# Softmax times values on one core: the values' spreads moved into the first two heads of a pass, and the last head's load cut into 2, 2, 2, 1, 1 rows

## The chip, the cores and the metric

One core of one Trainium2 chip (trn2). The metric is the device time of one execution in microseconds (us). It is somewhat longer than the span of the profile (first to last instruction): by 1.7 to 2.8 us in the runs of this study.

## The reference

```python
def setup_inputs():
    batch, n_heads, seq, head_dim = 8, 12, 1024, 64
    return {"scores": randn(batch, n_heads, seq, seq) float32,      # 403 MB
            "v": randn(batch, n_heads, seq, head_dim) float32}

def reference(scores, v):
    scores_max = np.max(scores, axis=-1, keepdims=True)
    attn = np.exp(scores - scores_max)
    attn = attn / (np.sum(attn, axis=-1, keepdims=True) + 1e-8)
    return np.matmul(attn, v).astype(np.float32)
```

96 heads, each a 1024 x 1024 block of scores and 1024 x 64 values.

## The kernel before

The program is a loop of 24 passes over four heads (numbered 0 to 3). A head has eight "rows" (`r`); a row is 128 queries by 1024 keys, and all eight lie in one buffer of 4 MB. For a row, ScalarE (ACT) takes the exponential (two rows in one instruction, one at a time for the last two rows of a pass), TensorE (PE) transposes eight 128 x 128 blocks into PSUM (the memory that it writes to), VectorE (DVE) copies them to SBUF (the core's working memory) (the "row copy", L273), and TensorE multiplies the eight blocks with the values and a column of ones (two rows later in the program). After four or eight rows DVE takes the reciprocals of the sums and multiplies. GpSimd (POOL) casts the values of four heads to 16 bits once per pass; DVE then *spreads* them, in four copies per head, into the layout that TensorE reads. The loop, abridged (`...` and the comments stand for what is left out):

```python
def heads(n0):
    for k in range(AHEAD):                     # four heads of a pass
        if k == 0:
            for s in range(S):                 # head 0's own four spreads
                spread_v(k, s)
        ...
        for r in range(R):                     # eight rows
            if r % EB == 0:
                ...                            # exp of two rows, ACT, L255
            psT = take(psT_bufs)               # four buffers
            for c in range(C):
                nc.tensor.transpose(...)       # PE, L267
            pt = take(pt_bufs)                 # four buffers
            copy = nc.vector.tensor_copy(out=pt[:], in_=psT[:])      # DVE, L273
            if k < AHEAD - 1 and r % (R // S) == 0:
                spread_v(k + 1, r // (R // S), copy)                 # DVE, L207
            if r == R - 1:
                load_next(k, n0)
            pending.append((n0, k, r, pt, st))
            if len(pending) > LAG:             # LAG = 2
                finish(pending.pop(0))         # PE, L145; DVE, L124 and L129
    while pending:
        finish(pending.pop(0))
    cast_v()                                   # POOL, L203
    last(n0)                                   # loads of heads 2, 3 and the values; store

# in last(), the last but one pass:
load(AHEAD - 2, BH - 2, (4, 4))
load(AHEAD - 1, BH - 1, (4,))
store(n0, AHEAD - T)
load(AHEAD - 1, BH - 1, (2, 1, 1), 4)
```

All transfers are issued by one queue (SP), in this order.

The softmax here doesn't subtract the row's maximum and nothing guards it: scores larger than these inputs give would overflow.

Of the kernel before, what the change touches and what calls it, by code (L numbers as in the profile page):

```python
# [14 lines left out]
def kernel(  # L15
# [12 lines left out]
    BH = B * H  # L28
    assert SQ % P == 0 and SK % P == 0
    R = SQ // P  # L30
# [5 lines left out]
    AHEAD = 4  # L36
    Q = P // AHEAD
    S = P // Q
# [54 lines left out]
    def take(bufs):  # L93
        k = turn.get(id(bufs), 0)
        turn[id(bufs)] = k + 1
        return bufs[k % len(bufs)]
# [4 lines left out]
    def after(a, b):  # L101

        tc.add_manual_dep(
            a.ins,
            b.ins.name,
            mybir.DependencyInfo(mybir.DependencyClass.NoSync, mybir.DependencyReason.DATA),
            reason="order",
        )

    def queue(dma):  # L110

        if queued:
            after(dma, queued[-1])
        queued.append(dma)

    def one(bh, n):
        return bh[bass.ds(n, 1)].rearrange("o p r d -> (o p) r d")

    def normalise(k, st, first, last):

        psO = psO_whole if k % 2 == 0 else psO_banks[first]
        psO = psO[:, :, 0 : G * M].rearrange("p b (g m) -> p b g m", m=M)
        recip = st["recip"][:, first:last]
        nc.vector.reciprocal(out=recip, in_=psO[:, :, :, D : D + 1])  # L124
        h = k % T
        for t in range(T):
            part = slice(t * W, (t + 1) * W)
            rows = st["out_sb"][h * W : (h + 1) * W, t, first * G : last * G, :]
            nc.vector.tensor_tensor(  # L129
                out=rows.rearrange("j (b g) d -> j b g d", g=G),  # L130
                in0=psO[part, :, :, 0:D],
                in1=recip[part].to_broadcast([W, last - first, G, D]),
                op=mybir.AluOpType.mult,
            )

    def finish(u):

        n0, k, r, pt, st = u
        b, g = r // G, r % G
        if r == 0:  # L140
            st["recip"] = take(rc_bufs)
            st["out_sb"] = out_bufs[k // T]
        bank = psO_whole[:, b] if k % 2 == 0 else psO_banks[b][:, 0]
        for c in range(C):
            nc.tensor.matmul(  # L145
                out=bank[:, g * M : (g + 1) * M],
                lhsT=pt[:, c * P : (c + 1) * P],
                rhs=st["vones"][:, c, 0:M],
                start=(c == 0),
                stop=(c == C - 1),  # L150
            )
        if k % 2 == 1:
            if g == G - 1:
                normalise(k, st, b, b + 1)
        elif r == R - 1:
            normalise(k, st, 0, R // G)
        if r == R - 1 and k == T - 1:
            store(n0, 0)

    def store(n0, k):  # L160

        rows = out_bh.rearrange("(m x) y -> m x y", x=P)
        dma = nc.sync.dma_start(
            out=rows[bass.ds((n0 + k) // T, 1)].rearrange("o x y -> (o x) y"),
            in_=out_bufs[k // T][:].rearrange("x t r d -> x (t r d)"),
        )
        for other in stores:
            apart(dma, other)
            apart(other, dma)
        apart(dma, dma)  # L170
        stores.append(dma)
        queue(dma)
# [8 lines left out]
    def load(k, n, parts=(R,), r=0, **cond):  # L181
        for rows in parts:
            queue(
                nc.sync.dma_start(  # L184
                    out=s_bufs[k][:, r : r + rows, :],
                    in_=one(sc_bh, n)[:, r : r + rows, :],
                    **cond,
                )
            )
            r += rows  # L190

    def load_v(n):

        rows = v_bh.rearrange("(m x) y -> m x y", x=P)
        queue(
            nc.sync.dma_start(  # L196
                out=v_sb[:].rearrange("x h s l d -> x (h s l d)"),
                in_=rows[bass.ds(n // AHEAD, 1)].rearrange("o x y -> (o x) y"),
            )
        )  # L200

    def cast_v():
        nc.gpsimd.tensor_copy(out=v_half[:], in_=v_sb[:])  # L203

    def spread_v(k, s, behind=None):

        copy = nc.vector.tensor_copy(  # L207
            out=vones_bufs[k][s * Q : (s + 1) * Q, :, 0:D].rearrange(
                "i (h l) d -> i h l d", l=L
            ),  # L210
            in_=v_half[k * Q : (k + 1) * Q, :, s],
        )
        if behind is not None:
            after(copy, behind)

    def load_next(k, n0):

        if k < AHEAD - 2:
            load(k, (n0 + (AHEAD + k)) % BH, cond=n0 < BH - AHEAD)

    def last(n0):


        before = queued[-1:]

        with tc.If(n0 < BH - 2 * AHEAD) as cmp:  # L226
            queued[:] = before
            load(AHEAD - 2, (n0 + (2 * AHEAD - 2)) % BH)
            load_v((n0 + 2 * AHEAD) % BH)
            load(AHEAD - 1, (n0 + (2 * AHEAD - 1)) % BH)  # L230
            store(n0, AHEAD - T)
        with cmp.Else():
            with tc.If(n0 < BH - AHEAD) as cmp2:
                queued[:] = before
                load(AHEAD - 2, BH - 2, (4, 4))
                load(AHEAD - 1, BH - 1, (4,))
                store(n0, AHEAD - T)
                load(AHEAD - 1, BH - 1, (2, 1, 1), 4)
            with cmp2.Else():
                queued[:] = before  # L240
                store(n0, AHEAD - T)

    def heads(n0):

        for k in range(AHEAD):
            if k == 0:
                for s in range(S):
                    spread_v(k, s)
            st = dict(vones=vones_bufs[k])
            for r in range(R):  # L250
                if r % EB == 0:
                    p_nat = take(p_bufs)
                    rows = 1 if k == AHEAD - 1 and r == R - EB else EB
                    for g in range(0, EB, rows):
                        nc.scalar.activation(  # L255
                            out=p_nat[:, g : g + rows, :].rearrange(
                                "p r (x v) -> p x r v", v=Q * L
                            ),
                            in_=s_bufs[k][:, r + g : r + g + rows, :].rearrange(
                                "p r (i x l) -> p x (r i) l", i=Q, l=L  # L260
                            ),
                            func=EXP,
                        )
                p_row = p_nat[:, r % EB, :].rearrange("p (h q l) -> p h l q", q=P, l=L)
                psT = take(psT_bufs)
                for c in range(C):
                    nc.tensor.transpose(  # L267
                        out=psT[:, c * P : (c + 1) * P],
                        in_=p_row[:, c // L, c % L, :],
                        identity=order16[:],  # L270
                    )
                pt = take(pt_bufs)
                copy = nc.vector.tensor_copy(out=pt[:], in_=psT[:])  # L273
                if k < AHEAD - 1 and r % (R // S) == 0:
                    spread_v(k + 1, r // (R // S), copy)
                if r == R - 1:
                    load_next(k, n0)
                pending.append((n0, k, r, pt, st))
                if len(pending) > LAG:
# [3 lines that stand above are left out]
        cast_v()  # L283
        last(n0)

    assert BH % AHEAD == 0 and BH >= 2 * AHEAD and SK == Q * S * C
# [5 lines left out]
    with tc.For_i(0, BH, AHEAD, iteration_sync="reg_based") as n0:  # L292
        queued.clear()
        heads(n0)
# [30 lines left out]
```

## Time and profile before

| | before |
|---|---|
| time, median of the first 3 runs | 1065.58 us (1065.39 to 1066.23) |
| span of the profiled run | 1064.0 us |
| bytes moved | 453 MB, 99.2% of 16 DMA engines' span |
| start of ACT on head 1 of the last pass | 1030.12 us |
| end of the last multiply | 1059.19 us |

I call the 29.06 us (of the unrounded times) between the last two rows the *tail*. It starts with the landing of head 1's scores (ACT waits for it). The prediction shows the page and the main views and how they are read. One more view is needed later, DVE's waits in the tail (columns: who waits, for whom, us in total, times, the longest):

```profile
DVE recip L124 <- PE psO L145: 0.7, 1, 0.7
DVE pt L273 <- PE L145: 0.2, 1, 0.2
DVE pt L273 <- PE psO L145: 0.2, 1, 0.2
```

### The profile page before, as it was taken

What the parts mean: (1) busy time and instruction counts of PE and PEld (TensorE: products, weight loads), DVE (VectorE), ACT (ScalarE), POOL (GpSimd) and SP (SyncE); (2) the same over time, 40 slices, a digit from 0 to 9 for tenths busy, and PEclk for the clock granted to TensorE, in tenths of its full rate; (3) what the DMA queues carried; (4) which work ended last, traced back from release to release, by engine and by line L of the source; (5) the groups of instructions that cost most, each with busy time, mean ns of one, the idle gap of its engine ahead of it and who ended that gap; (6) DMA issues with size and microseconds to landing.
All of it is one profiled execution on the core that took longest, in us unless ns stands there. A gap on an engine that the chain in (4) does not pass through costs nothing.

```text
span 1064.0 us, 32161 instructions
## 1 busy us (share of the span) xinstructions
PE 731.4 (69%) x12288; PEld 678.4 (64%) x12288; DVE 786.6 (74%) x1589; ACT 735.6 (69%) x432; POOL 48.1 (5%) x31
## 2 busy tenths in 40 slices
PE   2766766767766677677686776867666777666676
PEld 2665756667666667666575665767565666666675
DVE  3776876868768777677786776868768687687777
ACT  3766776666767668586676866667766668676685
POOL 0000000000000000000000000000000000000000
PEclk9888888878889888888988888888889788898989
DMA  9999999999999999999999999999999999999995
GB/s 397 431 418 434 426 433 434 433 434 432 432 434 432 425 443 430 429 431 428 433 431 436 432 434 434 431 434 424 441 427 434 432 426 435 432 432 428 440 425 236
DMA packets 24772, 453.06 MB, mean 426 GB/s; under 512 B 2752, under 2 KB 2752, under 8 KB 9152
## 3 DMA queue, kind: packets, MB, share of 16 engines
q1 hardware_dynamic: 24768, 453.00, 99.2%
q8 instruction: 4, 0.07, 0.0%
HBM read 436.21 MB, written 25.17 MB: 434 GB/s over the span
## 4 chain that ended last, share of the span: by engine, by line
DMA 81%; ACT 12%; issue 3%; ACTq 1%; PE 1%; DVE 0%; SPq 0%; PEld 0%; DVEq 0%
DMA s_nat<-in_scores_dram 81%; ACT p_nat L255 12%; PE psT L267 1%; ACTq L255 1%; ACTq L226 0%; ACTq L292 0%; PE psO L145 0%; DVE pt L273 0%; PE psO_whole L145 0%; SPq L184 0%; PEld L267 0%; ACTq L320 0%; DVE out_sb L129 0%; SPq L196 0%; PEld L145 0%
## 5 line engine op out<-in xcount | busy, mean ns | idle before, releaser
L255 ACT ACTIVATE p_nat<-s_nat 128x2048 f16<-128x2048 f32 (+1 forms) x408 | 704.8, 1799 | 228.1 <-DMA s_nat<-in_scores_dram 202.2
L267 PE MATMUL psT<-order,p_nat 128*128 128x128 f16 x6144 | 574.9, 246 | 269.9 <-ACT p_nat L255 263.9
L273 DVE COPY pt<-psT 128x1024 f16<-128x1024 f16 x768 | 515.8, 687 | 200.6 <-PE L267 109.4
L267 PEld LDWEIGHTS <-p_nat 128*128 128x128 f16 x6144 | 446.5, 123 | 298.3 <-ACT p_nat L255 295.7
L145 PEld LDWEIGHTS <-pt 128*128 128x128 f16 x6144 | 302.9, 107 | 81.0 <-DVE pt L273 77.7
L145 PE MATMUL psO<-vones,pt 128*128 128x65 f16 x3072 | 177.4, 201 | 53.9 <-DVE pt L273 50.2
L145 PE MATMUL psO_whole<-vones,pt 128*128 128x65 f16 x3072 | 189.9, 211 | 2.7 <-DVE pt L273 2.4
L207 DVE COPY vones<-v_half 32x512 f16<-32x512 f16 x384 | 109.4, 285 | 22.8 <-POOL v_half L203 6.0
L255 ACT ACT_TABLE_LOAD x24 | 30.8, 1283 | 89.8 <-DMA s_nat<-in_scores_dram 81.7
L203 POOL CAST v_half<-v_sb 128x2048 f16<-128x2048 f32 x25 | 47.4, 1896 | 1002.3 <-DVE vones L207 957.1
L129 DVE TENSOR_TENSOR out_sb<-psO,recip 64x256 f32<-64x256 f32 x192 | 81.1, 423 | 6.1
L129 DVE TENSOR_TENSOR out_sb<-psO_whole,recip 64x512 f32<-64x512 f32 x96 | 66.1, 688 | 3.0
L124 DVE RECIPROCAL recip<-psO 128x4 f32<-128x4 f32 x96 | 17.1, 178 | 34.4 <-PE psO L145 17.6
L124 DVE RECIPROCAL recip<-psO_whole 128x8 f32<-128x8 f32 x48 | 9.7, 203 | 4.5 <-PE psT L267 3.9
L71 DVE MEMSET vones<- 128x16 f16 x4 | 0.2, 72 | 0.8 <-PEq L309 0.8
L62 DVE CAST order<-ident 128x128 f16<-128x128 f32 x1 | 0.2, 227 | 0.4 <-POOL ident masks.py:199 0.4
masks.py:199 POOL TENSOR_SCALAR_AFFINE_SELECT ident<-ident 128x128 f32<-128x128 f32 x1 | 0.3, 295 | 0.1
masks.py:197 POOL MEMSET ident<- 128x128 f32 x1 | 0.2, 205 | 0.3 <-POOLq L309 0.3
L309 POOL MEMSET const-float32-0.0<- 128x1 f32 x1 | 0.1, 100 | 0.2 <-issue 0.2
L309 POOL MEMSET const-bfloat16-1.0<- 128x1 bf16 x1 | 0.1, 103 | 0.0
L309 POOL MEMSET const-uint8-127<- 128x1 uint8 x1 | 0.1, 103 | 0.0
L309 POOL MEMSET const-float32-1.0<- 128x1 f32 x1 | 0.1, 100 | 0.0
## 6 DMA issues: line engine op xcount, KB each, us to landing
s_nat<-in_scores_dram SPq DMA_DIRECT2D x96, 4096.0 KB, 35.8
v_sb<-in_v_dram SPq DMA_DIRECT2D x24, 1024.0 KB, 33.1
out_dram<-out_sb SPq DMA_DIRECT2D x48, 512.0 KB, 26.9
s_nat<-in_scores_dram SPq DMA_DIRECT2D x3, 2048.0 KB, 32.4
s_nat<-in_scores_dram SPq DMA_DIRECT2D x1, 1024.0 KB, 25.4
s_nat<-in_scores_dram SPq DMA_DIRECT2D x2, 512.0 KB
```

The lines of the kernel that those rows point to most:

```text
L62: nc.vector.tensor_copy(out=order16[:].rearrange("p (t j) -> p t j", t=T), in_=ident32[:].rearrange("p (j t) -> p t j", t=T),)
L71: nc.vector.memset(vo[:, :, D : D + 2], 1.0)
L124: nc.vector.reciprocal(out=recip, in_=psO[:, :, :, D : D + 1])
L129: nc.vector.tensor_tensor(out=rows.rearrange("j (b g) d -> j b g d", g=G), in0=psO[part, :, :, 0:D], in1=recip[part].to_broadcast([W, last ...
L145: nc.tensor.matmul(out=bank[:, g * M : (g + 1) * M], lhsT=pt[:, c * P : (c + 1) * P], rhs=st["vones"][:, c, 0:M], start=(c == 0), stop=(c ...
L203: nc.gpsimd.tensor_copy(out=v_half[:], in_=v_sb[:])
L207: copy = nc.vector.tensor_copy(out=vones_bufs[k][s * Q : (s + 1) * Q, :, 0:D].rearrange("i (h l) d -> i h l d", l=L), in_=v_half[k * Q : ( ...
L255: nc.scalar.activation(out=p_nat[:, g : g + rows, :].rearrange("p r (x v) -> p x r v", v=Q * L), in_=s_bufs[k][:, r + g : r + g + rows, :] ...
L267: nc.tensor.transpose(out=psT[:, c * P : (c + 1) * P], in_=p_row[:, c // L, c % L, :], identity=order16[:],)
L273: copy = nc.vector.tensor_copy(out=pt[:], in_=psT[:])
L309: nc = _bacc.Bacc("TRN2", target_bir_lowering=False, num_devices=1)
```

## The change

It wants to finish with the cast values earlier (so that the next cast and the next load of the values aren't held), to unload DVE in the last heads of a pass, and to let ACT start earlier on the very last head.

```diff
-                load(AHEAD - 1, BH - 1, (4,))
+                load(AHEAD - 1, BH - 1, (2,))
                 store(n0, AHEAD - T)
-                load(AHEAD - 1, BH - 1, (2, 1, 1), 4)
+                load(AHEAD - 1, BH - 1, (2, 2, 1, 1), 2)
...
-                if k < AHEAD - 1 and r % (R // S) == 0:
-                    spread_v(k + 1, r // (R // S), copy)
+                if k < 2 and r < 6:
+                    spread_v(1 + (k * 6 + r) // S, (k * 6 + r) % S, copy)
```

## The prediction

> **What bounds the kernel now.** I read the page first: the DMA row and the queue table, because 81% of the chain of work that ended last is one transfer, the load of the scores.
>
> ```profile
> DMA  9999999999999999999999999999999999999995
> GB/s 397 431 418 434 426 433 434 433 434 432 432 434 432 425 443 430 429 431 428 433 431 436 432 434 434 431 434 424 441 427 434 432 426 435 432 432 428 440 425 236
> q1 hardware_dynamic: 24768, 453.00, 99.2%
> DMA s_nat<-in_scores_dram 81%; ACT p_nat L255 12%; PE psT L267 1%; ACTq L255 1%; ACTq L226 0%; ACTq L292 0%; PE psO L145 0%; DVE pt L273 0%; PE psO_whole L145 0%; SPq L184 0%; PEld L267 0%; ACTq L320 0%; DVE out_sb L129 0%; SPq L196 0%; PEld L145 0%
> ```
>
> The reader is to see that 39 of 40 slices of the DMA row are full, at some 432 GB/s, and that only the last slice (26.6 us) is not. A pass over four heads moves 16.78 MB of scores, 1.05 MB of values and 1.05 MB of results, 18.87 MB; at 432 GB/s that is 43.7 us. The chain repeats at that distance (its long DMA pieces start at 405.63, 449.34 and 493.02 us). So 23 of the 24 passes are as long as their bytes.
>
> Second, busy time by stretch: one steady stretch, the end of the loads, and the tail.
>
> ```profile
> 500.00:544.00 44.00, 31.06 (x522) 28.84 (x520) 32.82 (x67) 30.91 (x19) 1.90 (x1) 0.85 1.00 430
> 1020.00:1046.00 26.00, 19.65 (x354) 17.69 (x352) 22.93 (x50) 23.28 (x14) 0.00 (x0) 0.93 0.99 425
> 1046.00:1064.00 18.00, 8.80 (x176) 7.69 (x176) 12.03 (x24) 7.50 (x5) 1.90 (x1) 0.87 0.35 145
> ```
>
> After the window come PE, PEld, DVE, ACT and POOL busy us, the clock, the DMA share and GB/s. In the steady stretch DVE is busy 32.8 of 44 us, so it has 11 us to spare per pass while DMA has none. In the last 18 us DMA is 35% busy: only here can compute set the end.
>
> Third, who waits on the issuing queue, to see what an earlier release could buy.
>
> ```profile
> SPq L184 <- ACT p_nat L255: 273.4, 47, 13.1
> SPq L163 <- DVE vones L207: 238.4, 23, 10.6
> SPq L196 <- POOL v_half L203: 97.3, 23, 5.6
> v_sb<-in_v_dram SPq DMA_DIRECT2D x24, 1024.0 KB, 33.1
> ```
>
> The load of the values waits for the cast, 4.2 us per pass (97.3/23). But that load lands 33.1 us after its issue (last row, from the table of DMA issues), while its own 1.05 MB is 2.4 us of transfer: it stands behind about 30 us of queued work. Issuing it 4 us earlier doesn't move its place in the queue.
>
> Fourth, the timeline of the end, of DVE, of ACT and of the queue.
>
> ```profile
> 1045.96 7.59 ACT L255 ACTIVATE p_nat<-s_nat 128x2048 f16<-128x2048 f32 x5 [1.14 <-DMA s_nat<-in_scores_dram]
> ...
> 1046.91 0.29 DVE L207 COPY vones<-v_half 32x512 f16<-32x512 f16 x1
> 1047.23 1.29 DVE L273 COPY pt<-psT 128x1024 f16<-128x1024 f16 x2
> 1048.55 0.29 DVE L207 COPY vones<-v_half 32x512 f16<-32x512 f16 x1
> 1048.87 1.90 DVE L273 COPY pt<-psT 128x1024 f16<-128x1024 f16 x3
> 1050.80 0.21 DVE L124 RECIPROCAL recip<-psO_whole 128x8 f32<-128x8 f32 x1
> ...
> 1056.69 0.69 DVE L273 COPY pt<-psT 128x1024 f16<-128x1024 f16 x1
> 1058.10 0.18 DVE L124 RECIPROCAL recip<-psO 128x4 f32<-128x4 f32 x1 [0.72 <-PE psO L145]
> 1058.31 0.88 DVE L129 TENSOR_TENSOR out_sb<-psO,recip 64x256 f32<-64x256 f32 x2
> ```
>
> ACT starts on the last head at 1045.96, 1.14 us after it was free, when the first four rows have landed, and then runs without a gap to 1053.55. DVE is behind it: from 1034.73 to 1057.38 it runs instruction after instruction with about 30 ns between them at most. The waits of DVE from 1032.8 on sum to 1.1 us, of which 0.7 us is the wait for the very last matmuls. So in the tail the end is set by DVE's backlog and not by ACT.
>
> **What the Trainium skill says.** "DMA: Bandwidth & Descriptors", Where 436 GB/s comes from, puts the ceiling of the 16 SBUF ports at 435.2 GB/s. The slices here read 424 to 443 with a mode of 432 to 434: the trace agrees, and there is nothing left to win in the steady loop. The same page, Queues, rings and completion order, says each DMA engine consumes descriptors in ring order; the 33.1 us of a 1 MB load agree. "Perfetto Trace Analysis", DMA Optimizations, says that splitting a transfer may let work start sooner if the DMA engines are generally idle. Here they are full, so a split can only reorder landings. "VectorE: DVE Perf Modes", The DRAIN you can't avoid, has the next operation wait until the pipe is empty unless it isn't held. Both are seen: back-to-back copies of the transposed rows start 0.61 us apart though one lasts 0.69, and a spread that stands between two of them stretches the distance to 1.03 us (1046.20 to 1047.23), so it costs 0.42 us there, and 0.32 us behind a multiply.
>
> **The change part by part.** *Spreads.* Nothing is removed: 12 copies of 32x512 at 0.285 us (109.4 us/384) remain per pass. Four each behind rows 0, 2, 4, 6 of heads 0, 1 and 2 become six each behind rows 0 to 5 of heads 0 and 1. In the steady loop this takes no time off the bound. The cast can run some 8 us earlier, until it meets the landing of its input (issued 966.59, landed 999.73; the cast ran at 1008.19). Gain: 0.
>
> In the last pass it counts. DVE has short waits in head 0 (0.25, 0.19 and 0.19 us before three row copies, 0.63 in all); the two extra spreads there cost 2 x 0.42 = 0.84 us, so about 0.2 us is carried into head 1. From head 1's first row copy (1032.82) to the end, eight spreads become six. Before, by their places: head 1 0.35 + 0.32 + 0.42 + 0.32, head 2 0.32 + 0.32 + 0.42 + 0.42, together 2.89 us. After: 0.35, about 0.25 (a wait of 0.16 us absorbs part), 0.32, and three at 0.42, 2.18 us. Saved 0.71 us, less the 0.2 carried in: 0.5 us at the end.
>
> *Parts of the last head.* In the last but one pass the load goes from 4, store, 2, 1, 1 rows to 2, store, 2, 2, 1, 1: same bytes, same last part. The first two rows land one 1 MB transfer (2.4 us) earlier, at about 1043.4 in place of 1045.86; ACT is busy with head 2 until 1044.82, so it starts 1.1 us earlier. Rows 2 and 3 land behind the store, where the store landed before (1047.19): ACT starts on them at 1047.2, against 1047.78. Rows 4 and 5 land as before (1049.63), where ACT started on them at 1049.74. So ACT meets the same landings from there and ends within 0.1 us of 1053.55. What this part buys is that DVE is not held at the head's first rows: before, row 0's transposes ended 0.65 us ahead of its copy (1048.83 against 1049.48), about the shift the spreads bring. It makes that shift safe and adds at most 0.1 us. One more transfer costs one issue of 0.33 us, 20 us ahead of the landing.
>
> Sum: 0.5 to 0.6 us off 1065.58, that is 1065.0.
>
> **The rivals.** (1) No effect at all: PE paces the tail, not DVE. With no spreads in head 2, DVE would copy seven rows in a row at 0.61 us, while PE needs about 0.70 us for a row's transposes and matmuls (1029.02, 1029.72, 1030.43 in head 0). For it: PE's lead in head 2 is only 0.3 to 1.6 us. Against: every copy there started within 30 ns of DVE becoming free. It would give 1065.3 to 1065.6.
> (2) The steady loop gets shorter, because the values' load no longer waits 4.2 us on the cast: 23 passes at even 1 us would be 1042. Against: the queue never runs dry, at 99.2%.
> (3) Six spreads in heads 0 and 1 make DVE late, so ACT frees the scores' buffers later and the loads are issued later. For it: head 0 also has its own four spreads. Against: DVE's 11 us spare per pass, and 25 us of queued transfers that hide a late issue. It would show as slices under 9 in the DMA row and a few us; I give it one chance in a hundred.
> (4) The store behind two rows in place of four makes a dry queue in the last but one pass. Against: the store was issued at 1023.68 while head 1 landed only at 1030.02 and two halves of head 2 still stood before it.
>
> **Range and chances.** The mechanism is worth 0 to 1 us; the three runs of before spread over 0.84 us (1065.39 to 1066.23), and the median of another kernel's runs moves by about as much. Predicted 1065.0, 8 in 10 between 1064.2 and 1065.9. Two per cent is 21 us, more than the whole tail: faster 0.005, same 0.99, slower 0.005.
>
> **What would show it right or wrong.** Right: DMA share about 99% and 43.7 us between passes as before; the queue's wait on the cast gone or far below 97 us; ACT starting on the last head near 1044.9 but ending near 1053.5; DVE's last row copy near 1056.1 in place of 1056.69. Wrong: that copy at its old place with DVE idle in the last two heads (PE paces, rival 1); ACT ending much earlier (the last rows land earlier than I hold); passes of another length (rivals 2 and 3).

## The result

| | before | changed |
|---|---|---|
| time, median of 6 runs | 1065.68 us (1065.39 to 1066.23) | 1066.65 us (1065.74 to 1067.01) |
| span of the profiled run | 1064.0 us | 1064.4 us |
| ACT starts on head 1 / head 3 of the last pass | 1030.12 / 1045.96 | 1030.52 / 1045.10 |
| ACT's end | 1053.55 | 1053.90 |
| last row copy / last multiply's end | 1056.69 / 1059.19 | 1057.38 / 1059.89 |
| tail | 29.06 us | 29.37 us |

The ratio is 1.0007, with a 95% interval from 0.9994 to 1.002. (Ratios here are the mean time of one kernel's fast runs over the mean of the other's of the same rounds, so not quite the ratio of the medians quoted.) By the 2% rule it is the same; 1066.65 lies above the predicted range, and the gain of half a us isn't there.

The loop is as it was. Page, and the same three stretches as in the prediction, of the changed kernel:

```profile
DMA  9999999999999999999999999999999999999995
q1 hardware_dynamic: 24912, 453.00, 99.2%
```

```profile
500.00:544.00 44.00, 30.42 (x522) 27.52 (x520) 33.33 (x70) 30.94 (x19) 1.90 (x1) 0.89 1.00 429
1020.00:1046.00 26.00, 19.49 (x355) 17.47 (x353) 23.32 (x51) 24.04 (x14) 1.89 (x1) 0.93 0.99 423
1046.00:1064.00 18.00, 9.51 (x184) 8.00 (x182) 11.96 (x23) 6.73 (x5) 0.00 (x0) 0.88 0.35 146
```

POOL's cast has moved out of the third stretch into the second: it now runs as soon as the values land (1000.26 after a landing at 1000.11 in the pass before, where it was 1008.19). The queue's wait on it is nearly gone, and the load of the values, issued earlier, only waits longer in the ring (36.7 in place of 33.1 us to its landing):

```profile
SPq L196 <- POOL v_half L203: 7.5, 2, 5.5
v_sb<-in_v_dram SPq DMA_DIRECT2D x24, 1024.0 KB, 36.7
```

In the chain of waits, the last long transfer of a pass lands at 1009.85 in place of 1009.47, a difference of 0.38 us over 23 passes, of which 0.3 us arises in a single pass. (That 0.4 us did not repeat: in two later traces with the same spreads, again_after and spread_only, head 1 starts at 1030.14 and 1030.15, as before the change.) The other 0.3 us of the later end lie in the tail. First ACT, before and then changed:

```profile
1030.12 14.70 ACT L255 ACTIVATE p_nat<-s_nat 128x2048 f16<-128x2048 f32 x8 [1.08 <-DMA s_nat<-in_scores_dram]
```

```profile
1030.52 16.48 ACT L255 ACTIVATE p_nat<-s_nat 128x2048 f16<-128x2048 f32 x9 [1.09 <-DMA s_nat<-in_scores_dram]
1047.68 1.92 ACT L255 ACTIVATE p_nat<-s_nat 128x2048 f16<-128x2048 f32 x1 [0.69 <-PE L145]
1050.09 3.81 ACT L255 ACTIVATE p_nat<-s_nat 128x2048 f16<-128x2048 f32 x3 [0.48 <-PE L267]
```

ACT now begins the last head directly behind head 2, as meant, but meets the landings of the later parts (rows 2 and 3 landed at 1047.58; the profile names PE in the brackets, whose work came last by its records). It ends 23.38 us after its start on head 1, against 23.43. Then DVE, from the copy of head 2's row 4 on, and its waits in the tail:

```profile
1046.74 1.88 DVE L273 COPY pt<-psT 128x1024 f16<-128x1024 f16 x3
1048.85 0.69 DVE L273 COPY pt<-psT 128x1024 f16<-128x1024 f16 x1 [0.23 <-PE L145]
1049.81 0.69 DVE L273 COPY pt<-psT 128x1024 f16<-128x1024 f16 x1 [0.27 <-PE L145]
1050.77 0.69 DVE L273 COPY pt<-psT 128x1024 f16<-128x1024 f16 x1 [0.27 <-PE L145]
1051.38 0.20 DVE L124 RECIPROCAL recip<-psO_whole 128x8 f32<-128x8 f32 x1
1051.73 0.69 DVE L273 COPY pt<-psT 128x1024 f16<-128x1024 f16 x1 [0.15 <-PE L145]
```

```profile
DVE pt L273 <- PE L145: 1.1, 5, 0.3
DVE recip L124 <- PE psO L145: 0.7, 1, 0.7
```

DVE did come free early, and then waited for TensorE before four copies. The copies start exactly 0.96 us apart. DVE has 0.3 us to spare each time, so something of TensorE has a period of 0.96 us per row, though matmuls and transposes of a row start 0.70 us apart when nothing holds them.

The trace also records each update of the semaphore by which TensorE tells of finished instructions, and DVE's copies wait on that semaphore (a counter that one engine raises and another waits on). A row has 16 matmuls and transposes, and each has a weight load; all 32 update it. Read from that record:

```
updates of TensorE's semaphore       before      changed
all                                   24579        24579
gaps of exactly 30 ns                 22520        22504
gaps under 29 ns                          0            0
```

So the updates leave one at a time, 30 ns apart at the least (two gaps are of 29 ns), and 32 x 30 ns = 0.96 us. This least distance doesn't follow the clock that TensorE is granted: before the change, where the trace has the granted clock at 0.5 of full speed, 4502 of 6168 gaps are of 30 ns as well, and none is under 29. The transposes of head 2's row 7 are drawn as ended at 1048.03 in the changed kernel, but the update that its copy waits for came at 1048.83, and the copy started at 1048.85. The three heads of the tail have 768 updates, 23.04 us, and before the change they took 24.80 us (1033.27 to 1058.07). The difference is time in which TensorE was held: 0.94 us, and 0.82 us at the very last row. The changed kernel has 2.08 us of such time: 0.3 us more. The longest holds are before the matmuls of head 1's rows 3, 5 and 7 (0.24, 0.12 and 0.44 us), each of which needs that row's copy, and head 1 is where DVE now does six spreads.

That is my theory, COUNTS: in the tail TensorE's completion counts leave no slack, so what holds TensorE in head 1 isn't made up later, and what DVE gains in head 2 it waits away. No run here removes updates and keeps the instructions; each transpose, matmul and weight load makes one, so a limit on updates and a limit on instructions completed can't be told apart, and "count" stands for both. The rivals: BACKLOG (the prediction's view, DVE's own work sets the end), PARTS (the new parts cost it) and LOADS (the difference comes from transfers, by chance).

### The profile page after: what moved, and what is told of

Same layout as the page of the kernel before. It is cut to its first block, busy times and chain, and to the rows that moved or that the text cites. A ratio compares the mean times of both kernels' runs of the same rounds, so it can differ in the third digit from the quotient of the medians.

```text
span 1064.4 us, 32188 instructions
## 1 busy us (share of the span) xinstructions
PE 737.3 (69%) x12288; PEld 682.5 (64%) x12288; DVE 786.2 (74%) x1589; ACT 735.8 (69%) x432; POOL 48.0 (5%) x31
## 3 DMA queue, kind: packets, MB, share of 16 engines
q1 hardware_dynamic: 24912, 453.00, 99.2%
## 4 chain that ended last, share of the span: by engine, by line
DMA 78%; ACT 13%; issue 3%; PE 2%; ACTq 1%; DVE 1%; PEld 1%; SPq 0%; DVEq 0%
DMA s_nat<-in_scores_dram 78%; ACT p_nat L255 13%; PE psT L267 1%; DVE pt L273 1%; ACTq L255 1%; PE psO_whole L145 1%; PE psO L145 0%; PEld L145 0%; PEld L267 0%; ACTq L226 0%; ACTq L293 0%; SPq L184 0%; ACTq L321 0%; DVE recip L124 0%; DVE out_sb L129 0%
## 5 line engine op out<-in xcount | busy, mean ns | idle before, releaser
L145 PE MATMUL psO<-vones,pt 128*128 128x65 f16 x3072 | 182.9, 205 | 60.0 <-DVE pt L273 58.6
## 6 DMA issues: line engine op xcount, KB each, us to landing
v_sb<-in_v_dram SPq DMA_DIRECT2D x24, 1024.0 KB, 36.7
```

The lines of the kernel that those rows point to most:

```text
L145: nc.tensor.matmul(out=bank[:, g * M : (g + 1) * M], lhsT=pt[:, c * P : (c + 1) * P], rhs=st["vones"][:, c, 0:M], start=(c == 0), stop=(c ...
```

## The experiments

All ran on one core. Their main numbers are in one table. The spans are means of runs, with those of the kernel before on the same chip beside them. "From head 1's first copy" is the time from the first row copy of head 1 in the last pass to the end of the last multiply; it leaves out what head 0 carries over.

| run | time, median (before) | span, mean (before) | tail | from head 1's first copy |
|---|---|---|---|---|
| before (first profile) | | | 29.06 | 26.37 |
| again_before | 1065.61 (1065.80) | 1063.97 (1064.00) | 29.10 | 26.35 |
| changed (first profile) | | | 29.37 | 26.70 |
| again_after | 1066.16 (1065.72) | 1064.26 (1063.87) | 29.62 | 26.70 |
| spread_only | 1066.25 (1065.72) | 1064.30 (1063.87) | 29.64 | 26.71 |
| parts_only | 1065.50 (1065.72) | 1063.62 (1063.87) | 28.85 | 26.18 |
| no_spread | 1065.32 (1065.72) | 1063.47 (1063.87) | 28.55 | 25.87 |
| two_more | 1068.87 (1065.76) | 1067.12 (1063.78) | 32.20 | 28.14 |
| even | 1065.66 (1065.76) | 1063.76 (1063.78) | 29.06 | 26.20 |
| late_mult | 1065.31 (1065.76) | 1063.26 (1063.78) | 28.53 | 25.85 |
| best | 1065.14 (1065.76) | 1063.06 (1063.78) | 28.38 | 25.50 |
| late_parts | 1065.03 (1065.80) | 1063.18 (1064.00) | 28.31 | 25.64 |
| best2 | 1065.25 (1065.80) | 1063.16 (1064.00) | 28.66 | 25.71 |

Except for two_more (ratio 1.003, interval 1.0015 to 1.0046) the intervals of the ratios all hold 1. It is the last column, which repeats within 0.03 us in the two kernels that were traced twice, that tells these kernels apart.

**again_after**: the changed kernel, unedited.

> The changed kernel once more, to see whether its about 1 us over before holds. 'Tail' is from the start of ACT on head 1 of the last pass to the end of the last multiply: 29.07 us before, 29.37 us in the first run of the changed kernel. Theory COUNTS (the tail is paced by TensorE's completion counts, one per 30 ns, 32 per row, so 0.96 us per row, and the six spreads of head 1 hold TensorE up): tail 29.3 to 29.45 again, time 0.2 to 0.5 us over before, and what was above that in the first six runs was chance. Theory LOADS (the first difference came from transfers in the loop): the start of the tail wanders by some tenths, the tail's length says nothing, and the time differs from before by another amount than the first time.

Span 0.39 us and time 0.44 us over before (the medians). The tail is 29.62, 0.17 us above the 29.45 that COUNTS allowed, so the range was missed: head 1's first copy came 0.26 us later, counted from ACT's start, than in the first trace. From that copy on it is 26.70 again. LOADS was right that the time would differ by another amount than the first time, but not that the tail says nothing: ACT starts on head 1 where it did before the change, and the loss behind head 1's first copy is there to the same 0.3 us. The first six runs had been 0.97 us over; their time beyond the span varied from 1.77 to 2.68 us, so about half of that excess isn't in the program's instructions.

**spread_only**: before, with the spreads of the change alone.

```diff
-                if k < AHEAD - 1 and r % (R // S) == 0:
-                    spread_v(k + 1, r // (R // S), copy)
+                if k < 2 and r < 6:
+                    spread_v(1 + (k * 6 + r) // S, (k * 6 + r) % S, copy)
```

> Only the spreads are moved, the parts of the last head are as before. COUNTS: the whole difference of the tail comes from here: tail 29.3 to 29.5, DVE waits of 0.2 to 0.3 us before the row copies around the end of head 2, time as the changed kernel. BACKLOG (my prediction: DVE's own work sets the end, two spreads fewer give 0.5 us): tail 28.4 to 28.6. PARTS (the new parts cost it): tail 28.5 to 29.1, below before.

Tail 29.64, from head 1's first copy 26.71: the whole loss. It is above the upper end I gave for COUNTS (29.5) by head 0's share, as in again_after. BACKLOG and PARTS both wanted less than before, and fall.

**parts_only**: before, with the new parts alone.

```diff
-                load(AHEAD - 1, BH - 1, (4,))
+                load(AHEAD - 1, BH - 1, (2,))
                 store(n0, AHEAD - T)
-                load(AHEAD - 1, BH - 1, (2, 1, 1), 4)
+                load(AHEAD - 1, BH - 1, (2, 2, 1, 1), 2)
```

> Only the parts of the last head are changed, the spreads are as before. COUNTS and BACKLOG: tail 28.95 to 29.15, as before, though ACT starts on the last head 0.8 to 1.1 us earlier: what waits is behind ACT. PARTS: tail 29.3 to 29.5, ACT's end on the last head later by as much.

Tail 28.85, 0.1 us below what was expected, and from head 1's first copy 0.19 us less than in the first trace of before (0.17 less than in the second). Before, ACT's first exponentials of the last head came late enough to hold TensorE's transposes for a moment (in the record of updates 0.09 and 0.11 us, about 1048.0); with two rows landing first these holds are gone. So this half of the change is a small gain, and the other half outweighs it.

**no_spread**: before, with the twelve spreads done once ahead of the loop; the results are wrong from the second pass on.

```diff
     cast_v()
+    for k in range(1, AHEAD):
+        for s in range(S):
+            spread_v(k, s)
     load_v(AHEAD)
...
-                if k < AHEAD - 1 and r % (R // S) == 0:
-                    spread_v(k + 1, r // (R // S), copy)
```

> Before, with the twelve spreads of heads 1 to 3 taken out of the loop and done once ahead of it (wrong results on purpose from the second pass on). BACKLOG: eight spreads at about 0.36 us fall out of DVE's chain behind head 1's start: tail 26.0 to 26.5. COUNTS: only TensorE's holds of 0.94 us in heads 1 and 2 can fall away: tail 28.1 to 28.5, with row copies 0.96 us apart and DVE waits before most of them.

Tail 28.55, a gain of 0.5 us where DVE's own work fell by some 2.9 us: BACKLOG is refuted, and the limit beneath it is COUNTS. It missed the range given for COUNTS (28.1 to 28.5) by a little, as the loads take over in the last head (the wait of 0.77 us below), and DVE waits before 8 of the 24 copies of the tail, not before most. DVE now waits in head 2 as the changed kernel did; the third and fourth of these copies are the first two rows of the last head:

```profile
1046.46 0.69 DVE L273 COPY pt<-psT 128x1024 f16<-128x1024 f16 x1 [0.27 <-PE psT L267]
1047.42 0.69 DVE L273 COPY pt<-psT 128x1024 f16<-128x1024 f16 x1 [0.27 <-PE psO_whole L145]
1048.88 0.69 DVE L273 COPY pt<-psT 128x1024 f16<-128x1024 f16 x1 [0.77 <-PE L145]
1049.78 0.69 DVE L273 COPY pt<-psT 128x1024 f16<-128x1024 f16 x1 [0.21 <-PE L145]
```

The first two start 0.96 us apart again. From head 1's first copy to head 2's last, 15 rows take 14.49 us, 0.97 us each.

**two_more**: before, with two matmuls of one column more in every row.

```diff
                 stop=(c == C - 1),
             )
+        for j in range(2):
+            nc.tensor.matmul(out=bank[:, 300 + j : 301 + j], lhsT=pt[:, 0:P],
+                             rhs=st["vones"][:, 0, 0:1], start=True, stop=True)
```

> Before, with two more matmuls of one column in every row, into columns of PSUM that nobody reads (results stay right). They add 4 completion counts to a row's 32, and by the start times of the trace (0.03 us for a matmul of 65 columns with its load) no more than 0.06 us of TensorE's work to its 0.70 us per row. COUNTS: 36 x 30 ns = 1.08 us per row, row copies that far apart where nothing else holds them; over the 24 rows of the tail 2.9 us, less what the 0.94 us of holds absorb, and some carried in from head 0: tail 31.0 to 32.5, time 2 to 3.5 us over before. If TensorE's work and not its counts pace (0.76 us per row, below the 0.96 seen): tail 29.0 to 29.4. BACKLOG: as before, 29.1.

Time 3.1 us over before, tail 32.20, as COUNTS had it, at nearly no work more. 1.8 us of it arises from head 1's first copy on, the rest is carried in (that copy is 4.06 us behind ACT's start, in place of 2.69). In the record of updates heads 1 and 2 end at 1043.71 and 1052.35: 8.64 us for eight rows of 36 updates, which is 8 x 36 x 30 ns to the last digit; all gaps of these two heads are of 30 ns, whether a transpose of 128 columns, a matmul of 65 or one of a single column stands behind them. The first copies of the last head, before which DVE waits, start 1.08 us apart (1051.65, 1052.73, 1053.81). Those two stretches in the view by stretch:

```profile
1035.10:1043.74 8.64, 6.67 (x134) 5.89 (x134) 7.98 (x17) 8.44 (x6) 0.00 (x0) 1.00 1.00 427
1043.74:1052.38 8.64, 7.28 (x154) 6.53 (x154) 8.03 (x17) 7.37 (x5) 1.49 (x1) 1.00 0.72 300
```

At the full granted clock (1.00), PE is drawn busy for 6.67 and 7.28 of 8.64 us and its weight loads for less: the two columns that stand for TensorE show room that isn't there.

**even**: before, with the spreads laid where DVE waits for TensorE.

```diff
-                if k < AHEAD - 1 and r % (R // S) == 0:
-                    spread_v(k + 1, r // (R // S), copy)
+                place = {0: 0, 1: 1, 2: 2, 3: 3, 4: 4, 5: 5, 11: 6, 12: 7,
+                         19: 8, 20: 9, 21: 10, 22: 11}          # row of the pass: spread
+                n = place.get(k * R + r)
+                if n is not None:
+                    spread_v(1 + n // S, n % S, copy)
```

> Spreads laid where DVE waits for TensorE: six behind rows 0 to 5 of head 0 as in the changed kernel, two behind rows 3 and 4 of head 1, four behind rows 3 to 6 of head 2; parts as before. COUNTS: TensorE is held less than before in heads 1 and 2: tail 28.4 to 28.9, near the 28.55 of the kernel without spreads, though DVE does the same six spreads behind head 1's start as in the changed kernel (29.4 to 29.6). If the number of spreads behind head 1's start decides and not their place: as the changed kernel, 29.4 to 29.6.

A miss in the size: tail 29.06. Head 0 carried 0.2 us over, which I hadn't put in. From head 1's first copy it is 26.20, half a us less than spread_only (26.71) with the same parts and just as many spreads (six) behind that point. So at the same number the place of the spreads decides.

**late_mult**: before, with the multiplies of the last head's first four rows held behind the last row's copy (an ordering edge, no other work).

```diff
         if k % 2 == 1:
-            if g == G - 1:
+            if g == G - 1 and k == AHEAD - 1 and b == 0:
+                held.append(st)
+            elif g == G - 1:
                 normalise(k, st, b, b + 1)
...
+                while held and r == R - 1:
+                    normalise(k, held.pop(), 0, 1, copy)       # its multiplies behind this copy
```

> Before, with the multiplies of the last head's first four rows held back until the last row's copy. In the trace of before the last row's transposes were complete at about 55.85 and the copy began at 56.69, behind those multiplies (0.89 us). COUNTS: the last copy starts 0.8 us earlier, the held multiplies then lie beside and a little beyond the last row's matmuls (0.72 us): tail 28.4 to 28.7, time 0.4 to 0.7 us below before. If the last copy waits for something else: tail 29.0 to 29.1.

Tail 28.53 and time 0.45 us below: as expected.

**best**: even, late_mult and the new parts together.

> The laid-out spreads of the run even, the late multiplies of late_mult and the new parts of the last head together. If the gains are in a row on one path: tail 27.7 to 28.2, time 0.9 to 1.4 us below before. If one takes the place of another: tail 28.4 or more.

Tail 28.38, between the two expectations; the 0.2 us carried over from head 0 are in it again. From head 1's first copy the three gains do add up: 0.17 (even), 0.52 (late_mult) and 0.19 us (parts_only) make 0.88, and 0.87 was measured.

**again_before**: the kernel before, unedited.

> The kernel before once more with a trace, to see how far the tail's length of 29.06 us repeats. COUNTS: 28.95 to 29.2, with head 1's first row copy 2.65 to 2.75 us after ACT's start on that head. If tails wander by half a us from run to run, the differences between the other runs mean little.

29.10, with head 1's first copy 2.76 us behind ACT's start (0.01 over the range): the tail repeats.

**late_parts**: late_mult and the new parts, with the spreads as before.

> The new parts of the last head and the late multiplies, with the spreads as before. COUNTS: parts_only's 0.2 us and late_mult's 0.5 us in a row: tail 28.2 to 28.45, as the run best, and without the 0.2 us that six spreads in head 0 carry into head 1.

Tail 28.31, as expected, and span 0.82 us below before. Its last lines show the held multiplies beside the last row's matmuls, where before there was a wait of 0.72 us:

```profile
1055.65 0.69 DVE L278 COPY pt<-psT 128x1024 f16<-128x1024 f16 x1 [0.15 <-PE L148]
1056.26 0.17 DVE L125 RECIPROCAL recip<-psO 128x4 f32<-128x4 f32 x1
1056.46 0.88 DVE L130 TENSOR_TENSOR out_sb<-psO,recip 64x256 f32<-64x256 f32 x2
1057.37 0.18 DVE L125 RECIPROCAL recip<-psO 128x4 f32<-128x4 f32 x1
```

**best2**: best, with four spreads in head 0 (rows 0, 2, 4, 6), four in head 1 (rows 0, 3, 4, 5) and four in head 2 (rows 3 to 6), by another `place` table.

> As the run best, but with four spreads in head 0 (rows 0, 2, 4, 6 as before), four in head 1 (rows 0, 3, 4, 5) and four in head 2 (rows 3 to 6). COUNTS: nothing is carried in from head 0, so that head 1's first row copy is back at 2.67 us behind ACT's start (2.88 in best), and head 2's spreads cost nothing: tail 28.1 to 28.3, if the fourth spread of head 1 holds TensorE for less than 0.1 us. If a spread costs DVE time wherever it stands: 28.6 or more.

A miss: tail 28.66, which is what was given for "a spread costs time wherever it stands", and head 1's first copy 2.95 us behind ACT's start, though head 0 is as before. 0.28 us of it is that copy's delay against the 2.67 us expected. Another 0.2 us, measured against best, lies behind it (25.71 against 25.50), with two spreads more there: the record of updates has one hold of 0.32 us in head 1 (at 1042.55) that is 0.05 us in best, so the condition that the fourth spread of head 1 holds TensorE for less than 0.1 us failed. What head 0 carries over isn't set by its number of spreads alone. The distance was 2.67 to 2.76 us in the traces with the old spreads or none (two_more aside), and 2.67, 2.87, 2.88, 2.93 and 2.93 in those with six in head 0. TensorE's granted clock (as a share of full speed) was 0.5 for 3.4 or 6.8 us about head 0, and that may be part of it: in best2 and spread_only (2.95, 2.93) this stretch ended only 0.4 to 0.5 us before ACT's start on head 1, in those at 2.67 to 2.76 it ended 1.4 to 3.5 us before. But again_after has 2.93 with the stretch ended 2.7 us before. I leave this share of 0.0 to 0.3 us open.

The version with the lowest median time is late_parts: 1065.03 us against 1065.80 us for before, ratio 0.9995 with an interval from 0.9981 to 1.0008. A gain isn't shown by the times, but the spans (1063.18 against 1064.00) and the tail agree.

## Why the prediction was wrong

By its own steps:

- *The loop is bound by its bytes; the cast's wait is worth nothing.* Right: the DMA row is the same and passes start 43.7 us apart. (The slices were read loosely: the first is 397 and the third 418, below the 424 named, and one at 443 is above the ceiling cited, so it's the usual 432 to 434 that agrees. That nothing is left to win rests on the 99.2%.) The wait on the cast fell from 97.3 to 7.5 us, and nothing came of it.
- *The new parts: ACT starts about 1.1 us earlier and ends within 0.1 us of where it did.* Right: head 3 starts 14.58 us after head 1 in place of 15.84 (1.25 us earlier, unrounded), and ACT's end, counted from head 1, differs by 0.05 us. The worth of at most 0.1 us was a little low (0.17 to 0.19 us in parts_only). The 0.65 us by which row 0's transposes were said to be ahead of their copy was read from drawn ends; in the record of updates it is 0.39 us (1049.09).
- *Head 0 carries about 0.2 us into head 1.* Right in size in again_after and spread_only (0.2 to 0.3), absent in the first trace. But best2, with four spreads in head 0, shows as much, so the reason given for it isn't shown.
- *"So in the tail the end is set by DVE's backlog and not by ACT."* This is the step that failed. I read it from DVE having no gaps. That shows that DVE was busy, not that it alone was slow: DVE's chain ran at about 1.0 us per row (24 rows from 1032.8 to 1057.4) above a limit of 0.96 us. With eight spreads gone, no_spread gained 0.5 us.
- *The saving of 0.71 us, spread by spread.* The sums were good for DVE alone: at head 2's row 7 its copy was 15.66 us after head 1's first, against 16.05, so 0.39 us had been saved, and 0.24 us more had gone into DVE's wait before that very copy. By head 3's row 3 it was 20.70 against 20.38. The saving was turned into waits for TensorE, and the delays of head 1 stayed (row 7's copy at 9.45 in place of 8.65, on which TensorE's matmuls of that row wait).
- *Rival (1), PE paces the tail,* was the right one, and I set it aside for two wrong reasons. The 0.70 us per row were start-to-start times; the completion counts need 0.96 us (two_more). And "every copy there started within 30 ns of DVE becoming free" holds just as well for a DVE that is hardly slower than TensorE. The sign that was named for it came: DVE idle before five copies of the tail, 1.1 us in all. Its time, 1065.3 to 1065.6, was too low too: I took it that moved spreads could then do no harm, where the six in head 1 held TensorE 0.3 us longer (spread_only).
- *The range.* Its upper end of 1065.9 took DVE's gain as the middle. The second set of runs (1066.16) is outside as well. Of the first set's 0.97 us, some 0.4 to 0.6 us is in the spans (mean 1064.4, against 1063.8 to 1064.0 of the kernel before in the three later sets), and the rest is time beyond the span, which no view shows.

## What to carry to other kernels

An engine without gaps is not yet the bound: ask what would hold it if it were faster, and compare rates, not gaps. For TensorE count instructions that report their completion, weight loads too, and look at the distance of the consumers' starts when they wait; the busy share and the starts don't show this limit. When two engines run within some per cent of each other, moving work earlier on one delays the other where it lands, and what is gained later may only become a wait.

## What the Trainium skill lacked or had wrong

- "TensorE: Matmul & The Clock Gate", The cost: per-tile semaphore tail, has the fact that I should have looked for: increments of matmuls serialize, at 26.3 ns each in its fit. It tells it of the tail behind packed tiles. The runs here show it as the pace of a long stream of ordinary 128 x 128 instructions, weight loads included, at 30 ns (22520 of 24578 gaps; 0.96 us per row of 32, 1.08 us per row of 36).
- "Perfetto Trace Analysis", Identifying the Most-Contended Engine, names MFU and the weight loads' busy share as the good measures for TensorE. The weight loads' share doesn't show a limit by completion counts (MFU was not worked out here): in two_more weight loads are busy for 5.89 of 8.64 us in a stretch in which TensorE's counts run without a gap. No page gives a measure for it.
